# Two of five gate/up pairs per layer as seven products of half blocks

## The chip, the cores and the metric

The kernel runs on one core of a Trainium2 chip. The metric is the device time of one execution in microseconds (us); a number given for a kernel is the median of several runs. The engines of the core are named as the profile names them: PE (TensorE, matmul), PEld (its weight loads), DVE (VectorE), ACT (ScalarE), POOL (GpSimd) and SP (SyncE, which here only issues transfers).

## The reference

A decoder trunk of two layers on 256 tokens of 1024 channels, all in float32. Each layer adds to the residual stream h first a mixer (a retention branch and a Mamba-2 branch, merged by gates), then a dense feed-forward part (FFN):

```
h = h + hybrid_mixer(rmsnorm(h, norm_mix_w[l]), w_in[l], ...)
h = h + swiglu(rmsnorm(h, norm_ffn_w[l]), w_gate_up[l], w_down[l])

def swiglu(h, w_gate_up, w_down):
    gu = h @ w_gate_up                       # 256 x 1024 by 1024 x 5632
    gate, up = jnp.split(gu, [D_FF], axis=-1)   # D_FF = 2816
    return (jax.nn.silu(gate) * up) @ w_down
```

A final rmsnorm follows the two layers. The change concerns only `h @ w_gate_up`.

## The kernel before

**Precision.** A float32 product is made of three matmuls: each factor is split into a high part, rounded to float32r, and a low part, the remainder. `mm3` (lines 339 to 342) adds high x high, high x low and low x high into one accumulator in PSUM. The weights are split on the fly: a piece of weights is brought by a transfer on SP's queue into a tile `raw` (128 partitions x up to 1024 elements, 512 KB); ACT copies it to the high part `wh` (line 324), DVE subtracts to get the low part `wl` (line 331). `feeder` (line 298) issues the loads in the order of the jobs, `splitter` (line 316) does the split. There are four `raw` buffers (RB) and six slots for split pieces (HB, the counter `hlS`). A raw buffer is free again when DVE has split it; a slot is free when PE has used the piece.

**The tokens** are split the same way: a norm (class `Norm`) scales the tokens, PE transposes them by `transposed` (line 375), ACT copies the high part out of PSUM into `xT` (line 387) and DVE subtracts the low part (line 388).

**Jobs of the FFN.** The 5632 columns of `w_gate_up` are five pairs of 512 gate columns and 512 up columns (NPAIR = 5, c = 0 to 4) and a last job with the 256 + 256 columns left. A job of 512 columns (`tm_job`, line 492) has four pieces of two k-blocks (256 of the 1024 rows each). For each of 8 k-blocks and of 2 blocks of 128 tokens it does one `mm3` of 512 columns: 48 matmuls, so 96 for a pair. Pair 0 is ordered so that the first token block goes ahead (`tm_pair`). When a token block of the gate is complete, ACT takes its Silu out of PSUM into a tile `sil` (line 1213); when that of the up part is, DVE multiplies (line 1221), and the product is transposed and split as operand `gu` of the down projection, `out_job(gu, ...)` on line 1249.

**The order of the work.** The program is written as cooperating generators. A planner (class `Flow`, line 61) runs them at build time with a cost for each instruction (`Op`) and hand-over times between engines. When an engine comes free in the plan, the ready operation with the lowest priority value `pr` is emitted next. This fixes the order of instructions on each engine. A job has number j: the split of its pieces has priority j - 0.7, its matmuls j + 0.5, its output work j. On the chip each engine works through its list in order and waits on semaphores.

**Buffers that the change touches.** Four accumulators in PSUM (`accS`), two transposition buffers (`trS`), three `sil` tiles, four `sx` tiles of 512 elements, two `seg` tiles of 1024 elements, four big tiles of tag D; `sx`, `seg` and D serve the mixer and are unused in the FFN.

Of the kernel before, what the change touches and what calls it, by code (L numbers as in the profile page):

```python
# [181 lines left out]
def trunk_kernel(  # L182
# [4 lines left out]
):  # L187
    nc = tc.nc
    HB, RB, TAIL, WARM = 6, 4, 5, 2
    cp = ctx.enter_context(tc.tile_pool(name="cp", bufs=1))  # L190
    wp = ctx.enter_context(tc.tile_pool(name="wp", bufs=HB))
    big = ctx.enter_context(tc.tile_pool(name="big", bufs=4))
# [19 lines left out]
    def tt(n, pr, out, in0, in1, op):  # L212
        return dve(n, pr, lambda: nc.vector.tensor_tensor(out=out, in0=in0, in1=in1, op=op))
# [14 lines left out]
    def pe(cost, pr, fn):  # L228
        return Op("pe", cost, fn, pr)
# [24 lines left out]
    def new_big(tag, dt, shape=(P, 4, SEQ)):  # L254
        return big.tile(list(shape), dt, tag=tag, name=tag, bufs=2 if tag == "xT" else 4)
# [12 lines left out]

    jobs = []
    specs = []  # L270

    def add_job(srcs):
        evs = []
        for src, k, n in srcs:
            ev = Event()
            evs.append(ev)
            specs.append((src, k, n, ev, len(jobs)))
        jobs.append(evs)

    def rows(w, k0, k, n0, n):  # L280
        return ([w[k0 : k0 + k * P, n0 : n0 + n].rearrange("(k p) n -> p k n", p=P)], k, n)
# [5 lines left out]
    def tm_srcs(w, n0, n=512, kper=2):  # L287
        return [rows(w, k0, kper, n0, n) for k0 in range(0, D, kper * P)]
# [7 lines left out]
    first_pieces, rest_pieces = Event(), Event()  # L296

    def feeder():
        for i, (src, k, n, ev, job) in enumerate(specs):
            if i == 2:  # L300
                fl.set(first_pieces)
                yield rest_pieces
            yield rawS

            def load():
                raw = new_raw()
# [7 lines left out]
            fl.spawn(splitter(raw, k, n, ev, job, fl.transfer(512 * k * n)))  # L314

    def splitter(raw, k, n, ev, job, landed):
        yield landed
        yield hlS
        m = k * n
        pr = job - 0.7  # L320
# [12 lines left out]

        wl = yield Op("dve", 1.04 * m + 69, split_l, pr)
        fl.release(rawS)
        fl.set(ev, (wh[:, :m].rearrange("p (k n) -> p k n", k=k), wl[:, :m].rearrange("p (k n) -> p k n", k=k)))


    def mm3(ps, lh, ll, rh, rl, first, last):
        nc.tensor.matmul(ps, lhsT=lh, rhs=rh, start=first, stop=False)  # L340
        nc.tensor.matmul(ps, lhsT=lh, rhs=rl, start=False, stop=False)  # L341
        nc.tensor.matmul(ps, lhsT=ll, rhs=rh, start=False, stop=last)  # L342

    class Operand:


        def __init__(self, n, tags):
            self.n, self.tags = n, tags
            self.parts = [None] * n
            self.ready = [[Event() for _ in range(NT)] for _ in range(n)]  # L350
# [21 lines left out]
            if self.tags[i] != "xT":  # L372
                fl.release(bigS[self.tags[i]])

    def transposed(src, n, dst, i, t, pr):
# [12 lines left out]
        yield tt(n * P, pr, dl, v, dh.bitcast(F32), ALU.subtract)  # L388
        fl.release(trS)
        fl.set(dst.ready[i][t])  # L390

    def power(ms, n, pr, tag, bufs):
        r = sp.tile([P, 2], F32, tag=tag, name=tag, bufs=bufs)
# [18 lines left out]
    class Norm:  # L412


        def __init__(self, w):
# [11 lines left out]
        def half(self, t, n, pr):  # L427

            nsl = slice(n * 512, (n + 1) * 512)
            fl.spawn(self.square(t, n, pr))  # L430
            wb = yield self.wb[n]
            r = yield self.rstd[t]
            yield silS
            xn = new_sil()
            yield stt(512, pr, xn, h[t][:, nsl], r, wb, ALU.mult, ALU.mult)
            self.left -= 1
            if not self.left:
                self.free()
            yield from transposed(xn, 4, self.xT, n, t, pr)
            fl.release(silS)  # L440

        def square(self, t, n, pr):
            nsl = slice(n * 512, (n + 1) * 512)
# [53 lines left out]
    def tm_pair(xT, *members):  # L497

        return tm_jobs(xT, members, [(m, t, k) for t in range(NT) for m, n in ((0, 8), (1, 4)) for k in range(n)]
                       + [(1, t, k) for k in range(4, 8) for t in range(NT)])  # L500

    def fm_job(xT, post):

# [92 lines left out]
    def add_layer_jobs(l):  # L596
        for kind, *at in MIXER:
            if kind == "v":
                add_job(tm_srcs(w_in[l], C_V + 512 * at[0], kper=1 if l == at[0] == 0 else 2))
            elif kind == "gr":  # L600
                add_job(tm_srcs(w_in[l], C_DT + 352 * at[0], 352))
            elif kind == "q":
                add_job(fm_srcs(w_in[l], C_Q + DK * at[0]))
            elif kind == "k":
                add_job(fm_srcs(w_in[l], C_K + DK * at[0]))
            elif kind == "bc":
                add_job(fm_srcs(w_in[l], C_X + 256 * (8 + 2 * at[0] + at[1])))
            elif kind == "xs":
                add_job(fm_srcs(w_in[l], C_X + 256 * (2 * at[0] + at[1])))
            elif kind == "g":  # L610
                add_job(tm_srcs(w_in[l], C_G + 512 * at[0]))
            elif kind == "z":
                add_job(tm_srcs(w_in[l], C_Z + 512 * at[0]))
            elif kind == "gs":
                add_job(tm_srcs(w_in[l], C_GS + 512 * at[0]))
            else:
                add_job(out_srcs({"ret": ret_out, "ssd": ssd_out, "wo": w_o}[kind][l]))
        for c in range(NPAIR):
            add_job(tm_srcs(w_gate_up[l], 512 * c))
            add_job(tm_srcs(w_gate_up[l], FF + 512 * c))  # L620
# [31 lines left out]
    def layer(l, mix, nxt):  # L652
# [517 lines left out]


        mT = Operand(2, ["A", "A"])
        ffn = Norm(norm_ffn_w[l])

        def ssd_post(t, n, ps, j):
            nsl = slice(n * 512, (n + 1) * 512)
# [10 lines left out]
        def ssd_job():  # L1187
            for i in range(2):
                xT.drop(i)
            fl.spawn(ffn.start(at_job[0]))  # L1190
            return out_job(yz, 16, ssd_post)

        run["ssd"] = ssd_job
# [33 lines left out]
        def both_post(t, ps, j):  # L1227
# [6 lines left out]
            yield from transposed(s, n // P, gu, NPAIR, t, j)  # L1234
            fl.release(silS)

        for c in range(NPAIR):
            sg_ev = [Event() for _ in range(NT)]
# [7 lines left out]
        for i in range(2):  # L1246
            ffn.xT.drop(i)
        fl.spawn(nxt.start(at_job[0]))
        yield from out_job(gu, FF // P, add_to(nxt))

# [201 lines left out]
```

## Time and profile before

| what | value |
|---|---|
| median of 3 runs | 1292.29 us (1292.07 to 1292.76) |
| the profiled execution | 1291.82 us |
| its span in the profile | 1290.1 us |
| PE busy | 1279.6 us, 99% |
| DVE busy | 860.5 us, 67% |
| ACT busy | 739.4 us, 57% |
| bytes moved | 237.65 MB, mean 184 GB/s |

The span runs from the first to the last record of the profile; the device time holds 1.7 us more. Engines work at once, so the busy shares add up to more than 100%. Matmuls are pipelined: one is shown with 0.39 us, but the next starts 0.23 us after it. A bracket at the end of a row tells how long the engine idled before it and what ended the idling. The FFN of the first layer runs from 461 to 650 us, that of the second from 1097 us to the end.

### The profile page before, as it was taken

Reading aid. Unit: us, or ns where it says so; the run is one execution under the profiler, and the core shown is the slowest. Engines: PE = TensorE matmul, PEld = TensorE weight load, DVE = VectorE, ACT = ScalarE, POOL = GpSimd, SP = SyncE. Lnnn points to the kernel's source line nnn. Section 1 sums busy time; section 2 is a strip of 40 time slices with the busy share of each in tenths; the row PEclk is TensorE's granted clock in tenths of the full one; section 3 lists DMA queues with packets and bytes.
Section 4 is the critical chain, followed back from the end, with each engine's and each line's share of the span. In section 5 each row is a group of like instructions: output and inputs, shape, how many; then the busy total and the mean of one; then the engine's idle time right before and its main releaser. Section 6 shows DMA issues by size and latency. Waiting matters only on the chain.

```text
span 1290.1 us, 16966 instructions
## 1 busy us (share of the span) xinstructions
PE 1279.6 (99%) x6324; PEld 1075.5 (83%) x6324; DVE 860.5 (67%) x1163; ACT 739.4 (57%) x1086; POOL 35.1 (3%) x57
## 2 busy tenths in 40 slices
PE   9999999999999999999999999999999999999997
PEld 7888888888888888888888988888888888888886
DVE  5875788878575665554478658878876756755544
ACT  5755676886365354444377556966955634544432
POOL 1000000000010000000010000000000100000000
PEclk9999999999999999999999999999999999999999
DMA  7757565556565566665566575656555553766551
GB/s 241 219 168 219 160 192 159 175 194 194 159 216 200 163 198 201 186 194 181 159 199 188 169 205 156 187 182 183 190 168 179 198 210 131 237 187 190 186 188 57
DMA packets 129013, 237.65 MB, mean 184 GB/s; under 512 B 7818, under 2 KB 59906, under 8 KB 128803
## 3 DMA queue, kind: packets, MB, share of 16 engines
q1 hardware_dynamic: 127458, 232.16, 58.1%
q0 software_dynamic: 1472, 4.42, 1.2%
q8 instruction: 49, 0.80, 0.3%
q14 instruction: 34, 0.27, 0.1%
HBM read 235.43 MB, written 1.11 MB: 183 GB/s over the span
## 4 chain that ended last, share of the span: by engine, by line
PE 87%; DVE 4%; ACT 3%; issue 3%; DMA 3%; POOL 0%; SPq 0%; POOLq 0%; DVEq 0%; ACTq 0%
PE acc L340 21%; PE acc L342 21%; PE acc L341 21%; PE acc L521 9%; PE acc L522 5%; PE tr L382 2%; PE yps L1060 2%; DVE wl L331 2%; DMA raw<-in_w_in_dram 1%; PE acc L524 1%; ACT wh L324 1%; ACT seg L1028 1%; PE sm L819 1%; DMA seg<-acs 1%; PE tr L954 0%
## 5 line engine op out<-in xcount | busy, mean ns | idle before, releaser
L331 DVE TENSOR_TENSOR wl<-raw,wh 128x1024 fp32r<-128x1024 f32 (+2 forms) x432 | 514.4, 1194 | 307.9 <-ACT wh L324 305.6
L324 ACT ACTIVATE wh<-raw 128x1024 fp32r<-128x1024 f32 (+2 forms) x432 | 443.8, 1035 | 358.3 <-PE acc L342 277.9
L340 PE MATMUL acc<-wh,xT 128*128 128x512 f32 (+1 forms) x896 | 348.6, 389 | 0.7 <-ACT wh L324 0.5
L341 PE MATMUL acc<-wl,xT 128*128 128x512 f32 (+1 forms) x896 | 343.1, 383 | 0.8 <-DVE wl L331 0.7
L342 PE MATMUL acc<-wh,xT 128*128 128x512 f32 (+1 forms) x896 | 343.0, 383 | 0.0
L521 PE MATMUL acc<-xT,wh 128*128 128x512 f32 x560 | 203.8, 401 | 0.0
L341 PEld LDWEIGHTS acc<-wl,xT 128*128 128x128 f32 x896 | 168.5, 188 | 31.9 <-DVE wl L331 1.9
L340 PEld LDWEIGHTS acc<-wh,xT 128*128 128x128 f32 x896 | 168.5, 188 | 31.8 <-ACT wh L324 0.9
L342 PEld LDWEIGHTS acc<-wh,xT 128*128 128x128 f32 x896 | 168.2, 188 | 31.8
L522 PE MATMUL acc<-xT,wl 128*128 128x256 f32 x640 | 167.2, 281 | 0.0
L522 PEld LDWEIGHTS acc<-xT,wl 128*128 128x128 f32 x640 | 120.9, 189 | 6.9
L521 PEld LDWEIGHTS acc<-xT,wh 128*128 128x128 f32 x560 | 105.5, 188 | 21.3
L340 PE MATMUL acc<-wh,A 128*128 128x512 f32 x192 | 76.7, 400 | 0.0
L216 DVE SCALAR_TENSOR_TENSOR cb<-ca,cv,cb 128x255 f32<-128x255 f32 (+1 forms) x144 | 68.4, 478 | 10.9 <-ACT cb L206 9.8
L342 PE MATMUL acc<-wh,A 128*128 128x512 f32 x192 | 74.9, 390 | 0.0
L341 PE MATMUL acc<-wl,A 128*128 128x512 f32 x192 | 74.8, 390 | 0.0
L340 PE MATMUL acc<-wh,Y 128*128 128x512 f32 x176 | 70.7, 402 | 0.0
L342 PE MATMUL acc<-wh,Y 128*128 128x512 f32 x176 | 68.7, 391 | 0.0
L341 PE MATMUL acc<-wl,Y 128*128 128x512 f32 x176 | 68.6, 390 | 0.0
L340 PE MATMUL acc<-wh,C 128*128 128x512 f32 x128 | 50.6, 395 | 0.0
L342 PE MATMUL acc<-wh,C 128*128 128x512 f32 x128 | 49.9, 390 | 0.0
L341 PE MATMUL acc<-wl,C 128*128 128x512 f32 x128 | 49.8, 389 | 0.0
(141 smaller groups left out, 1295.1 us busy)
## 6 DMA issues: line engine op xcount, KB each, us to landing
raw<-in_w_in_dram SPq DMA_DIRECT2D x188, 512.0 KB, 4.4
raw<-in_w_gate_up_dram SPq DMA_DIRECT2D x80, 512.0 KB, 3.7
raw<-in_w_down_dram SPq DMA_DIRECT2D x44, 512.0 KB, 3.3
raw<-in_ret_out_dram SPq DMA_DIRECT2D x32, 512.0 KB, 4.0
raw<-in_ssd_out_dram SPq DMA_DIRECT2D x32, 512.0 KB, 3.3
raw<-in_w_in_dram SPq DMA_DIRECT2D x24, 352.0 KB, 3.2
seg<-acs SPq DMA_DIRECT2D x16, 512.0 KB, 5.0
raw<-in_w_o_dram SPq DMA_DIRECT2D x16, 512.0 KB, 3.3
```

Of the source, the lines that this page charges most:

```text
L216: return Op("dve", 1.04 * n + 130, lambda: nc.vector.scalar_tensor_tensor(out=out, in0=in0, scalar=scalar, in1=in1, op0=op0, op1=op1), pr)
L324: nc.scalar.activation(out=wh[:, :m], in_=raw[:, :m], func=AF.Copy)
L331: nc.vector.tensor_tensor(out=wl[:, :m], in0=raw[:, :m], in1=wh[:, :m].bitcast(F32), op=ALU.subtract)
L340: nc.tensor.matmul(ps, lhsT=lh, rhs=rh, start=first, stop=False)
L341: nc.tensor.matmul(ps, lhsT=lh, rhs=rl, start=False, stop=False)
L342: nc.tensor.matmul(ps, lhsT=ll, rhs=rh, start=False, stop=last)
L382: nc.tensor.transpose(out=ps[:, j * P : (j + 1) * P], in_=src[:, j * P : (j + 1) * P], identity=ident)
L521: nc.tensor.matmul(a, lhsT=wh[:, k % 4, fsl], rhs=x[:, k % 4, :, :], start=k == 0, stop=False)
L522: nc.tensor.matmul(a[:, :SEQ], lhsT=wl[:, k % 4, fsl], rhs=xh[:, k % 4, :], start=False, stop=False)
L524: nc.tensor.matmul(a, lhsT=wh[:, k % 4, fsl], rhs=x[:, k % 4, :, :], start=False, stop=True)
L819: nc.tensor.matmul(ps[:, :SEQ], lhsT=k[:, b, :P], rhs=q[:, b, :], start=b == 0, stop=b == 1)
L1060: nc.tensor.matmul(ps[:, i * HD : (i + 1) * HD], lhsT=sg[:, i, :], rhs=xdt[:, i * HD : (i + 1) * HD], start=True, stop=True)
```

## The change

In pairs 2 and 4 of each layer (`WINO`) the pair is computed as one 2 x 2 block product by Winograd's form of Strassen's scheme. X is the normed input: its two token blocks are the block rows, the two halves of its 1024 channels the block columns (X11, X12, X21, X22, each 128 tokens by 512 channels). W has the block rows "first and second 512 channels" and the block columns "gate" and "up" (W11, W12, W21, W22, each 512 x 512). Instead of eight block products there are seven, of four k-blocks each, done in this order (`PRODUCTS`), each with three matmuls per k-block:

| product | token operand | weight operand | accumulator |
|---|---|---|---|
| 11 | X11 | W11 | u |
| t1 | X21 - X22 | t1 = W11 + W12 | v |
| t2 | (X21 - X22) - X11 | t2 = t1 + W22 | u, on top of 11 |
| 22 | X12 + that | W22 | c1 |
| t3 | X11 - X21 | t3 = W12 + W22 | u, on top |
| 21 | X12 | W21 | c2 |
| t4 | X22 | t4 = t2 + W21 | u, on top |

- **Weights** (`add_wino`, `wino_sums`): each block comes in two pieces of 1024 elements. W11 is loaded into `seg` tiles and becomes t1, t2 and t4 in place, by three DVE additions per piece. W12 stays in its raw buffer and becomes t3, not by DVE but by a transfer from POOL's queue that reads W22 once more from DRAM and adds it into the tile (`ADDED`). All seven operands are split, so a pair has 14 splits of 1024 elements, where it had 8. The raw buffer of W22 is kept until it is split and t2 is made, that of W21 until it is split and t4 is made.
- **Tokens** (`Norm.sums`, `transposed(..., plain)`): once per layer, behind the FFN's norm, ACT makes four unsplit copies of the transposed tokens in `sx`, DVE makes four differences and sums of 512 elements, each of which is split by ACT and DVE into tiles of tag D.
- **Outputs** (`wino_job`): while PE goes on with other accumulators, ACT copies u out of PSUM after 11, after t2 and after t3; the next product into u waits for that copy. DVE makes two additions for the up part of token block 0, one for its gate part, one for the up part of token block 1. Silu, product, transposition and split follow as before.
- **Order of the splits**: all pieces of the program now take their slots in the order of a list (`turns`).

The core of the diff (the token sums, the output additions and the plumbing of `feeder` and `splitter` are left out):

```diff
+    WINO, ADDED = (2, 4), ("t3",)
+    def wino_sums(i, job, evs, turn, held, part):
+        pr = job - 0.7
...
+        def add(raw, q):
+            yield Op("pool", 1050, lambda: nc.gpsimd.dma_start(
+                out=raw.rearrange("p (k n) -> p k n", k=2), in_=part[q][i], accum_op=ALU.add), pr)
+            yield fl.transfer(512 * D) + 1000.0
...
+        def plus(q, x, raw, src):
+            if q in ADDED:
+                yield from add(x, src)
+            else:
+                w = yield raw
+                yield tt(D, pr, x, x, w, ALU.add)
+            fl.set(used[q])
...
+        x = yield held["11", i]
+        yield from split(x, "11")
+        yield from plus("t1", x, w12, "12")
+        yield from split(x, "t1")
+        yield from plus("t2", x, w22, "22")
+        yield from split(x, "t2")
+        yield from plus("t4", x, w21, "21")
+        yield from last(x, "t4", segS)
...
+    def wino_job(norm, post):
+        def product(q, box, first):
+            xh, xl = yield norm.ops[q]
+            if first:
+                yield accS
+            for k in range(4):
+                wh, wl = yield evs[q][k // 2]
...
+                yield pe(3 * mm_cost(512), j + 0.5, emit)
+                if k % 2:
+                    fl.release(hlS)
...
+        yield from product("11", u, True)
+        fl.spawn(copied(u, silS, new_sil, u1e))
+        yield from product("t1", v, True)
+        u1 = yield u1e
+        yield from product("t2", u, False)
+        fl.spawn(copied(u, sxS, new_sx, u2e))
+        yield from product("22", c1, True)
+        u2 = yield u2e
...
+        yield from product("t3", u, False)
+        fl.spawn(copied(u, sxS, new_sx, u3e))
+        yield from product("21", c2, True)
...
+        u3 = yield u3e
+        yield from product("t4", u, False)
...
         for c in range(NPAIR):
+            if c in WINO:
+                yield from wino_job(ffn, wino_post(c))
+                continue
```

## Rows read from the trace of the kernel before

**Rows 1.** The page: span, then busy us, share and instructions of each engine.
```profile
span 1290.1 us, 16966 instructions
PE 1279.6 (99%) x6324; PEld 1075.5 (83%) x6324; DVE 860.5 (67%) x1163; ACT 739.4 (57%) x1086; POOL 35.1 (3%) x57
```

**Rows 2.** The page: granted TensorE clock in 40 slices, tenths of full speed.
```profile
PEclk9999999999999999999999999999999999999999
```

**Rows 3.** Waits of PE in the whole run: us in total, times, longest.
```profile
PE idle L1332 <- DVE zeros L1305: 1.5, 1, 1.5
PE acc L341 <- DVE wl L331: 0.7, 2, 0.5
PE tr L382 <- DVE sil L216: 0.5, 2, 0.3
PE acc L340 <- ACT wh L324: 0.5, 1, 0.5
PE acc L340 <- DVE Y L213: 0.2, 1, 0.2
```

**Rows 4.** Busy PE, PEld, DVE, ACT, POOL; clock, DMA share, GB/s: pairs 1, 2; 2.
```profile
484.60:507.30 22.70, 22.70 (x105) 18.82 (x104) 12.36 (x13) 10.77 (x12) 0.00 (x0) 1.00 0.69 209
507.30:530.00 22.70, 22.70 (x105) 18.81 (x104) 12.26 (x13) 10.77 (x12) 0.00 (x0) 1.00 0.64 185
...
1142.60:1165.30 22.70, 22.70 (x105) 18.82 (x105) 12.27 (x14) 10.77 (x12) 0.00 (x0) 1.00 0.66 185
```

**Rows 5.** Timeline of PE as pair 2 begins: start us, us, instruction.
```profile
507.55 0.39 PE L341 MATMUL acc<-wl,xT 128*128 128x512 f32 x1
507.77 0.39 PE L342 MATMUL acc<-wh,xT 128*128 128x512 f32 x1
508.00 0.60 PE L382 MATMUL tr<-cst,sil 128*128 128x128 f32 x4
508.36 0.48 PE L340 MATMUL acc<-wh,xT 128*128 128x512 f32 x1
508.67 0.40 PE L341 MATMUL acc<-wl,xT 128*128 128x512 f32 x1
```

**Rows 6.** Timeline of ACT: three splits back to back, then two in pair 1.
```profile
460.42 2.94 ACT L324 ACTIVATE wh<-raw 128x1024 fp32r<-128x1024 f32 x3
...
504.80 1.06 ACT L324 ACTIVATE wh<-raw 128x1024 fp32r<-128x1024 f32 x1 [1.66 <-PE acc L342]
507.52 1.06 ACT L324 ACTIVATE wh<-raw 128x1024 fp32r<-128x1024 f32 x1 [1.66 <-PE acc L342]
```

**Rows 7.** Timeline of DVE between pairs 1 and 2.
```profile
505.89 1.23 DVE L331 TENSOR_TENSOR wl<-raw,wh 128x1024 fp32r<-128x1024 f32 x1 [1.49 <-ACT wh L324]
507.03 1.28 DVE L213 TENSOR_TENSOR sil<-acc,sil 128x512 f32<-128x512 f32 x2
...
509.75 1.34 DVE L213 TENSOR_TENSOR C<-tr,C 128x512 fp32r<-128x512 f32 x2
```

**Rows 8.** Groups by line: operation, tiles, shapes, count, busy us, mean ns.
```profile
L213 DVE TENSOR_TENSOR seg<-seg,cbm 128x1024 f32<-128x1024 f32 x16 | 19.5, 1220 | 2.9 <-ACT seg L206 2.9
L213 DVE TENSOR_TENSOR tail<-tail,xdt 128x512 f32<-128x512 f32 x8 | 5.5, 687 | 0.1
L206 ACT ACTIVATE sil<-acc 128x512 f32<-128x512 f32 x10 | 6.0, 599 | 5.8 <-PE acc L342 5.5
```

**Rows 9.** Landing of the gate/up loads from SP, then of POOL's 512 KB transfers (L405).
```profile
DMA to landing us min/median/max: 2.8/3.7/6.5
...
DMA to landing us min/median/max: 4.2/4.6/6.6
```

**Rows 10.** Timeline at the start of layer 0's FFN, transposes of the second token block.
```profile
467.36 0.63 PE L382 MATMUL tr<-cst,sil 128*128 128x128 f32 x4 [0.25 <-DVE sil L216]
...
468.93 0.68 DVE L213 TENSOR_TENSOR xT<-tr,xT 128x512 fp32r<-128x512 f32 x1
...
471.03 0.39 PE L340 MATMUL acc<-wh,xT 128*128 128x512 f32 x1
```

More of the change, by code (lines that the diff above doesn't have):

```diff
@@ new lines, in new_raw_seg, with holder, land, then @@
+    def new_raw_seg():
+        return new_seg("raws").rearrange("p h i -> p (h i)")
+    def holder(ev):
+        def land(raw, landed):
+            yield landed
+            fl.set(ev, raw)
+        return land
+    def then(land, gens):
+        def run(raw, landed):
+            for g in gens:
+                fl.spawn(g)
+            yield from land(raw, landed)
+        return run
+    def wino_sums(i, job, evs, turn, held, part):
+        pr = job - 0.7
+        def split(raw, q):
+            wh, wl = yield from split_piece(raw, D, turn[q, i], pr)
+            fl.set(evs[q][i], tuple(a.rearrange("p (k n) -> p k n", k=2) for a in (wh, wl)))
+        def add(raw, q):
+            yield Op("pool", 1050, lambda: nc.gpsimd.dma_start(
+                out=raw.rearrange("p (k n) -> p k n", k=2), in_=part[q][i], accum_op=ALU.add), pr)
+            yield fl.transfer(512 * D) + 1000.0
+        def last(raw, q, sem):
+            yield from split(raw, q)
+            fl.release(sem)
+        w12, w22, w21 = (held[q, i] for q in ("12", "22", "21"))
+        used = {q: Event() for q in ("t1", "t2", "t3", "t4")}
+        def plus(q, x, raw, src):
[5 more added lines that the diff above has]
+            fl.set(used[q])
+        def side(ev, q, *sums):
+            raw = yield ev
+            yield from split(raw, q)
+            for a in sums:
+                yield used[a]
+            fl.release(rawS)
+        def third():
+            raw = yield w12
+            if "t1" not in ADDED:
+                yield used["t1"]
+            yield from plus("t3", raw, w22, "22")
+            yield from last(raw, "t3", rawS)
+        fl.spawn(side(w22, "22", *(q for q in ("t2", "t3") if q not in ADDED)))
+        fl.spawn(third())
+        fl.spawn(side(w21, "21", *(q for q in ("t4",) if q not in ADDED)))
+        x = yield held["11", i]
[6 more added lines that the diff above has]
+        yield from last(x, "t4", segS)
@@ L298, in feeder @@
     def feeder():
-        for i, (src, k, n, ev, job) in enumerate(specs):
+        for i, (src, k, n, job, (sem, alloc), land) in enumerate(specs):
             if i == 2:
@@ L313, in feeder, with split_piece @@
             raw = yield Op("sp", 450, load, job)
-            fl.spawn(splitter(raw, k, n, ev, job, fl.transfer(512 * k * n)))
-    def splitter(raw, k, n, ev, job, landed):
-        yield landed
+            fl.spawn(land(raw, fl.transfer(512 * k * n)))
+    def split_piece(raw, m, turn, pr):
+        if turn:
+            yield turns[turn - 1]
         yield hlS
-        m = k * n
-        pr = job - 0.7
+        fl.set(turns[turn])
         def split_h():
@@ L334, in splitter, with land, mm3 @@
         wl = yield Op("dve", 1.04 * m + 69, split_l, pr)
[L335 to L342, printed above, removed]
+        return wh[:, :m], wl[:, :m]
+    def splitter(turn, k, n, ev, job):
+        def land(raw, landed):
+            yield landed
+            wh, wl = yield from split_piece(raw, k * n, turn, job - 0.7)
+            fl.release(rawS)
+            fl.set(ev, tuple(a.rearrange("p (k n) -> p k n", k=k) for a in (wh, wl)))
+        return land
+    def mm3(ps, lh, ll, rh, rl, first, last, **kw):
+        nc.tensor.matmul(ps, lhsT=lh, rhs=rh, start=first, stop=False, **kw)
+        nc.tensor.matmul(ps, lhsT=lh, rhs=rl, start=False, stop=False, **kw)
+        nc.tensor.matmul(ps, lhsT=ll, rhs=rh, start=False, stop=last, **kw)
     class Operand:
@@ L388, in transposed @@
         yield tt(n * P, pr, dl, v, dh.bitcast(F32), ALU.subtract)
+        fl.set(dst.ready[i][t])
+        if plain:
+            yield sxS
+            x = new_sx("plain")
+            yield act(n * P, pr, x.rearrange("p (j t) -> p j t", j=n), v, AF.Copy, psum=True)
+            fl.set(plain, x)
         fl.release(trS)
-        fl.set(dst.ready[i][t])
     def power(ms, n, pr, tag, bufs):
@@ L412, in trunk_kernel, with __init__ @@
     class Norm:
-        def __init__(self, w):
+        def __init__(self, w, sums=False):
+            self.plain = [[Event() if sums else None for _ in range(NT)] for _ in range(2)]
+            self.ops = {q: Event() for q in PRODUCTS}
             self.xT = Operand(2, ["xT", "xT"])
@@ L1245, in layer @@
         yield from tm_job(ffn.xT, both_post)
-        for i in range(2):
-            ffn.xT.drop(i)
+        ffn.drop()
         fl.spawn(nxt.start(at_job[0]))
```

119 lines of the change are left out of this document (111 added, 8 removed).

## The prediction

> **What bounds the kernel now.** I read the busy times first: TensorE (PE) is busy 1279.6 of 1290.1 us, at the full granted clock in every slice [rows 1, 2]. A busy PE is not yet a PE that waits for nothing, so the waits of PE come next: all that it waited for other engines is 3.4 us in the whole run, 1.5 of it before the first job [rows 3]. So what takes work off PE shortens the span, as long as the other engines still deliver in time. For that the stretch of one pair counts, not the average: each gate/up pair lasts 22.70 us with PE busy throughout, DVE 12.3 and ACT 10.8, alike in both layers (two pairs of the first layer, one of the second) [rows 4]. The PE timeline shows why: matmuls start every 0.227 us, and a set of four transposes takes 0.45 us beyond that (507.77 to 508.67, less two such steps) [rows 5]. 96 x 0.227 + 2 x 0.45 = 22.7. The ACT and DVE timelines show the supply: a split starts on ACT when PE frees a slot of the six (504.80, 507.52: one per 2.72 us, the 12 matmuls of a piece) and its second half on DVE ends 2.3 us later [rows 6, 7]. Five pieces thus lie finished ahead of PE, and PE never sees a split in this stretch.
>
> **What goes.** A changed pair has 7 products of 4 k-blocks with 3 matmuls each, 84 for 96 of the same shape, and the same transposes. 12 x 0.227 = 2.72 us less PE per pair; two pairs in each of two layers make 48 matmuls, **-10.9 us**. The pair lasts 20.0 us.
>
> **What comes on the other engines.** Per changed pair 14 pieces are split for 8: six more, and six weight sums on DVE (t1, t2, t4 for two halves). Back to back a split takes DVE 1.14 us (505.89 to 507.03) and ACT 0.94 (2.94 for three less one's own 1.06, halved) [rows 6, 7]. A sum has no row of its own; the 1024-wide tensor_tensor on three SBUF tiles took 1.22 us, as the split does singly [rows 8], so I take 1.14 back to back. Four output adds of 512 (0.69 singly, 0.61 back to back, three SBUF tiles or one PSUM [rows 7, 8]) come to DVE, three copies out of PSUM (0.60 as the Silu there [rows 8]) to ACT. DVE: 20 x 1.14 + 4 x 0.61 + the 2.6 of two products and two second halves that it does per pair now [rows 7] = 27.8 us, against 20.0 of PE. ACT: 14 x 0.94 + 3 x 0.5 + 4 x 0.5 = 16.7, which fits. So inside such a pair DVE is the engine with too much to do, by 7.8 us. Over the pair and the ordinary one beside it DVE needs 27.8 + 11.7 = 39.5 of 42.7 us. The question is whether it can be spread.
>
> **DVE by time.** Let T be the moment when PE starts a changed pair after an ordinary one. Slots come free at T-13.6, -10.9, -8.2, -5.4, -2.7, 0 and then, as PE eats half pieces of 6 matmuls, every 1.36 us. By T five pieces (11 twice, t1 twice, t2) can be split and the four sums of t1 and t2 made: 9 x 1.14 = 10.3 of the 13.6 us, in which DVE has nothing else but its last ordinary splits. The pieces for it are there: the four raw buffers hold both halves of w12 and w22, whose loads (3.7 us median [rows 9]) follow the last ordinary splits, done by T-13.9; the halves of w11 have buffers of their own. From T: the 2.6 us of the pair before, nine splits and two t4 sums, 11 x 1.14 = 12.5, together 15.1. One gap: w21 needs a raw buffer that the split of w22 frees at about T+4.4, so it lands near T+8.5, when DVE has done 2.6 + 5 x 1.14 = 8.3. That ends the last split at about T+15.6. PE needs it when 13 halves are through, T + 13 x 1.36 + 0.9 = T+18.6: **3 us of margin**. The first piece of the next job and the four output adds bring DVE to T+15.6 + 1.1 + 2.4 = 19.1, before T+20.0; two of the adds free the accumulators that the next job starts with. In the ordinary pair behind, DVE has 2.6 + some 16 x 1.14 = 21 us for 22.7, and from T+27 on the slots hold it back again, so pair 4 starts as pair 2 did; after pair 4 come the shared last piece and the down projection, with ordinary splits alone.
>
> **The accumulator u** is written by 11, t2, t3 and t4 in turn, and copied out between them: 11, t1 then t2; t2, 22 then t3; t3, 21 then t4. Each copy has one product's 2.72 us. On ACT at most one split is in front of it (1.06 + 0.60 = 1.7, plus the hand-over), so I take nothing; behind it stand only splits with 6 us to spare. With three splits ahead, 3 x 0.94 + 0.6 = 3.4, PE would stand 0.7 plus hand-overs, about 1.1 us.
>
> **The adding transfer** on POOL: no row shows one. Plain 512 KB transfers from POOL landed after 4.2 to 6.6 us [rows 9]. The lower bound is those; the upper I set at 13.2, twice the longest, since the tile is read as well as written. The first is issued when the t1 sum is made, about T-9.9, the second T-7.2. ACT wants t3 at T+5 to 6.5 in its order; PE is not late until the second comes after T+10.8 (start of its product half at T+13.2 less 2.4 for the two halves of the split). At 6.6 they land by T-0.6: nothing. I take that end, the nearest kind of transfer. At 13.2 side by side nothing either; one after the other the second lands at T+16.5. POOL has nothing else queued there. DMA carries 1.05 MB more in such a pair: 5.2 MB over 20 us is 262 GB/s against 185 at a DMA share of 0.64 [rows 4], a share of 0.91. Landings get later; with the longest load seen, 6.5 us [rows 9], w21's first split ends about T+13.9 and its product starts at T+14.5. That still holds.
>
> **FFN start.** Four plain copies (0.60) on ACT, four differences and four splits of 512 (8 x 0.61 DVE, 4 x 0.5 ACT) per layer. Two copies come ahead of the second token block's norm, 1.2 us at worst on its chain; xT of it is ready at 469.61 and PE takes it at 471.03, 1.4 us later [rows 10]. DVE and ACT idle for about 3 us just behind, and the results are not used for two pairs. I take 0.2 us per layer for transposes queued on PE at their planned place, like the 0.25 there now [rows 10]; bounds 0 and 1.2. In each changed pair I take 0.3 us for the same thing, the longest such wait of the run [rows 3], as DVE comes to its output products without slack; bounds 0 and 2.2 (two late copies of u).
>
> **The sum** from the profiled execution: 1291.82 - 10.9 + 2 x 0.2 + 4 x 0.3 = 1282.5. That execution lies 0.47 below the median of the runs, so the predicted median is **1283.0 us**.
>
> **A rule that speaks against it.** DVE, by the rows, is needed 27.8 us in a stretch that PE would do in 20.0. The Trainium skill, Perfetto Trace Analysis, section Identifying the Most-Contended Engine, says to optimize the engine with the highest occupancy, and its Optimization Strategy section adds that this engine can change between regimes. By that rule, with no spreading between regimes, it is the second rival below; the trace bears out only its first half (PE is that engine now), and shows no stretch of this kind.
>
> **Rivals.** (1) Half gained: u is copied late twice a pair, 2.2 us each time around, or DVE lags as much. -10.9 + 0.4 + 4 x 2.0 = -2.5 at worst, -6.5 for half of that: 1285.8 to 1289.8. For it: engines work in a fixed order, and DVE has little slack. Against: 3 us of margin above. (2) Slower, DVE sets the pair. The place is the nine pieces of work before T: what of it is not done by then is added to DVE's 15.6 behind T. Three us are free by the margin, from 5.7 us on (3.0 + 2.72) the pair is longer than now. With all four sums and the t1 and t2 splits left (7 x 1.14 = 8 us) the loss is 8 - 5.7 = 2.3 per pair, 1292.3 + 9 = 1301; with no spreading at all, 27.8 - 22.7 = 5.1 per pair, 1313. For it: raw buffers are held through two uses. Against: the slot times. (3) Slower by the adding transfer: each us that the second lands after T+10.8 stops ACT, which splits in order, and so PE; past T+13.5 the kernel loses. At T+16.5: 5.7 - 2.7 = 3.0 per pair, 1304. (4) No change: PE pays in hand-overs what it saves, 1292. That needs 2.7 us in each pair, where now it shows 0.
>
> **Chances.** Forecast (1281 to 1285.5) 0.62, (1) 0.20, (2) 0.06, (3) 0.06, (4) 0.06. The low end of the range is no stall at all, 1281.4 less half the spread of the runs, 1280.9; the high end takes in most of (1), 1289.0. Below 1289.7 (0.2%, about what a measurement of this kernel tells from no change) lie the forecast and (1): faster 0.82; within 0.2% the most of (4): 0.05; slower (2), (3) and the rest of (4), 0.13.
>
> **What will show it.** Matmul groups with xT or D fall by 48 in all; a pair of 20.0 to 20.5 us with DVE busy nearly throughout, and a normal one of 22.7 behind it; in the waits of PE at most some tenths at the transposes, nothing on a split; ACT waiting for no adding transfer, and these landed in under 13 us. The prediction is wrong if PE waits for DVE's or ACT's splits by whole microseconds in a changed pair, or for u's copy, or if ACT waits for the adding transfer; and if the mixer's stages, which the change leaves, last longer.

## The result and the profile after

The changed kernel takes 1281.36 us (median of 4 runs, 1280.49 to 1282.07) against 1292.53 us of the kernel before on the same chip (4 runs): a ratio of 0.9911, 95% interval 0.9897 to 0.9925. The prediction was 1283.0 us, range 1280.9 to 1289.0. The profiled execution took 1282.07 us; the sum in the prediction had 1282.5 for it.

The page of the changed kernel, span and busy us with instruction counts, stands against [rows 1]:

```profile
span 1280.3 us, 17056 instructions
...
PE 1268.4 (99%) x6276; PEld 1065.7 (83%) x6276; DVE 931.6 (73%) x1243; ACT 774.5 (60%) x1138; POOL 43.1 (3%) x65
...
PEclk9999999999999999999999999999999999999999
```

PE has 48 instructions fewer and 11.2 us less to do; DVE has 71 us more and ACT 35, and the span is 9.8 us shorter all the same. The granted clock is full in every slice, as in [rows 2], so none of this is the clock.

The waits of PE in the whole run of the changed kernel (us in total, times, longest), against [rows 3]:

```profile
PE tr L486 <- DVE sil L214: 1.6, 4, 0.9
PE idle L1572 <- DVE zeros L1545: 1.5, 1, 1.5
PE acc L445 <- DVE wl L428: 0.7, 2, 0.5
PE acc L444 <- ACT wh L421: 0.6, 1, 0.6
PE acc L444 <- DVE Y L214: 0.3, 1, 0.3
```

The first line is the new one, 1.6 us at four transposes of output products (0.5 us in layer 0, 1.1 in layer 1). The `tr` wait of [rows 3] on line 382 (0.5 us, at the FFN's start) is gone. The other four are those of before.

Windows of the first layer's pairs 1 to 4 in the changed kernel; the columns are those of [rows 4] (busy PE, PEld, DVE, ACT, POOL, then clock, DMA share, GB/s):

```profile
484.40:507.10 22.70, 22.40 (x103) 18.32 (x102) 17.83 (x19) 10.54 (x12) 2.50 (x2) 1.00 0.77 212
507.10:527.10 20.00, 20.00 (x93) 16.55 (x92) 19.41 (x21) 16.17 (x19) 0.00 (x0) 1.00 0.53 175
527.10:549.80 22.70, 22.70 (x105) 18.72 (x104) 20.71 (x21) 12.21 (x14) 2.98 (x3) 1.00 0.92 272
549.80:569.80 20.00, 20.00 (x93) 16.56 (x93) 19.44 (x21) 16.53 (x19) 0.00 (x0) 1.00 0.60 197
```

This is the whole change in four lines. Pairs 2 and 4, by seven products, last 20.0 us with PE busy throughout; the ordinary pairs keep their 22.7. Look at the DVE column: 12.3 us per pair before, now 17.8 in the pair ahead of the first changed one, 19.4 in it, 20.7 in the ordinary pair between the two, 19.4 in the next. The 27.8 us of a changed pair don't stand in one window; they are spread over the neighbours. In the changed pairs DVE has 0.6 us free, in the ordinary pair 3 between them, where it does most (20.7 us), 2.0.

### The profile page after: what moved, and what is told of

The parts are those of the page before. It is cut to its first block, busy times and chain, and to the rows that moved or that the text cites. A ratio compares the mean times of both kernels' runs of the same rounds, so it can differ in the third digit from the quotient of the medians.

```text
span 1280.3 us, 17056 instructions
## 1 busy us (share of the span) xinstructions
PE 1268.4 (99%) x6276; PEld 1065.7 (83%) x6276; DVE 931.6 (73%) x1243; ACT 774.5 (60%) x1138; POOL 43.1 (3%) x65
## 4 chain that ended last, share of the span: by engine, by line
PE 89%; DVE 4%; DMA 3%; issue 2%; ACT 2%; SPq 0%; POOLq 0%; POOL 0%; DVEq 0%; ACTq 0%
PE acc L444 21%; PE acc L446 21%; PE acc L445 21%; PE acc L740 10%; PE acc L741 6%; PE tr L486 2%; DVE wl L428 2%; PE yps L1282 2%; PE acc L743 1%; DMA raw<-in_w_gate_up_dram 1%; ACT wh L421 1%; DMA raw<-in_w_down_dram 1%; DMA raw<-in_w_in_dram 1%; PE tr L1176 1%; PE ips L1269 1%
## 5 line engine op out<-in xcount | busy, mean ns | idle before, releaser
L428 DVE TENSOR_TENSOR wl<-raw,wh 128x1024 fp32r<-128x1024 f32 (+2 forms) x424 | 503.8, 1193 | 216.8 <-ACT wh L421 214.5
L421 ACT ACTIVATE wh<-raw 128x1024 fp32r<-128x1024 f32 (+2 forms) x424 | 434.6, 1034 | 285.9 <-PE acc L446 193.0
L444 PE MATMUL acc<-wh,xT 128*128 128x512 f32 (+1 forms) x816 | 317.1, 389 | 1.0 <-ACT wh L421 0.6
L445 PE MATMUL acc<-wl,xT 128*128 128x512 f32 (+1 forms) x816 | 311.7, 382 | 0.8 <-DVE wl L428 0.7
L446 PE MATMUL acc<-wh,xT 128*128 128x512 f32 (+1 forms) x816 | 311.6, 382 | 0.0
L444 PEld LDWEIGHTS acc<-wh,xT 128*128 128x128 f32 x816 | 153.3, 188 | 28.9 <-ACT wh L421 1.0
L445 PEld LDWEIGHTS acc<-wl,xT 128*128 128x128 f32 x816 | 153.4, 188 | 28.8 <-DVE wl L428 1.9
L446 PEld LDWEIGHTS acc<-wh,xT 128*128 128x128 f32 x816 | 153.2, 188 | 28.7
L217 DVE SCALAR_TENSOR_TENSOR cb<-ca,cv,cb 128x255 f32<-128x255 f32 (+1 forms) x144 | 68.5, 479 | 10.9 <-ACT cb L207 9.8
L421 ACT ACTIVATE wh<-raws 128x1024 fp32r<-128x1024 f32 x32 | 33.6, 1057 | 29.4 <-PE acc L446 24.8
```

Of the source, the lines that this page charges most:

```text
L217: return Op("dve", 1.04 * n + 130, lambda: nc.vector.scalar_tensor_tensor(out=out, in0=in0, scalar=scalar, in1=in1, op0=op0, op1=op1), pr)
```

## Experiments

Each kernel differs from the changed one by the edit shown; the order of the instructions was planned anew each time, with the same costs. Ratios are against the kernel before, on the same chip.

**1. The token sums alone.**

```
-    WINO, ADDED = (2, 4), ("t3",)
+    WINO, ADDED = (), ("t3",)
```

> All five pairs are computed the ordinary way again; the token copies and token sums at the start of each FFN and the new order of taking slots stay, their results unused. Theory A (the gain is 48 matmuls, everything else is hidden): the time of the kernel before, 1292.5 us, plus 0 to 0.4. Rival (the token sums cost what the prediction allowed at most): up to 1294.9, 1.2 us per layer. Rival (part of the gain comes from another order of the work, not from the matmuls): clearly below 1292, by up to 1 us.

Measured: 1291.39 us against 1292.85, ratio 0.9989 (0.998 to 0.9998). With no changed pair the kernel is not slower but 1.5 us faster, by the interval 0.3 to 2.6. If the token sums cost anything, the rest of the edit makes up for it, and a small part of the gain (one eighth, uncertain by nearly its own size) does not come from the matmuls taken out. Its waits of PE have no `tr` wait longer than 0.2 us. The trace does not say where all of it comes from: its span is 1.6 us shorter than that of the kernel before, but 0.7 of this lies ahead of the first FFN (the first instruction of its norm on POOL starts at 454.95 for 455.67), where every engine goes through the same instructions in the same order in both kernels. That much is a difference between two executions.

**2. All four weight sums on DVE** (no adding transfer).

```
-    WINO, ADDED = (2, 4), ("t3",)
+    WINO, ADDED = (2, 4), ()
```

> The sum t3 is made by DVE as the other three; no adding transfer. That puts 2 x 1.14 = 2.3 us more on DVE per changed pair, which then needs 30.1 us. Theory A: both sums are made before the pair starts, in a stretch of 22.7 us where DVE is busy 17.8 in the changed kernel, so they cost PE nothing: 1281 to 1282.5. Rival B (DVE is full at 19.4 of 20.0 us in a changed pair, so what is put on it is paid by PE): 4 x 2.3 = 9 us more, 1290.5. Between: if the w22 buffer is held longer and w21 comes later, up to 1 us per pair, 1285.

Measured: 1288.12 us against 1292.85, ratio 0.9966 (0.9953 to 0.9978). Theory A, mine, missed by 6 us. Two sums of 1.14 us in place of the transfer cost the kernel more than half of its gain. The windows of pairs 2, 3 and 4 in this kernel say where:

```profile
507.10:527.10 20.00, 20.00 (x93) 16.56 (x92) 19.34 (x21) 15.95 (x19) 0.00 (x0) 1.00 0.53 164
527.10:549.80 22.70, 22.12 (x102) 18.06 (x101) 19.88 (x21) 11.20 (x15) 0.00 (x0) 1.00 0.66 226
549.80:569.80 20.00, 17.37 (x79) 13.70 (x78) 19.30 (x20) 14.37 (x17) 0.00 (x0) 1.00 0.49 156
```

Pair 2 is untouched, although its sums are on DVE as well; it is pair 4 that PE cannot keep. So the 3 us of margin inside a pair, by which I had judged, are not the bound. The waits of PE, whole run:

```profile
PE acc L444 <- ACT sil L207: 3.6, 2, 1.8
PE tr L486 <- DVE sil L214: 3.6, 5, 1.5
```

Twice (once per layer) PE stands 1.8 us for a copy of u, the place of rival (1). The chain runs backward from it: PE's matmul, ACT's copy of u, the splits on ACT ahead of that copy, the sum of t2 that the first of them needs. Timelines (start us, us, instruction, in brackets the idle time before it), first PE and ACT:

```profile
559.89 0.50 PE L444 MATMUL acc<-wh,D 128*128 128x512 f32 x1 [1.80 <-ACT sil L207]
```

```profile
549.76 1.06 ACT L421 ACTIVATE wh<-raws 128x1024 fp32r<-128x1024 f32 x1 [3.48 <-DVE raws L214]
...
554.52 1.05 ACT L421 ACTIVATE wh<-raws 128x1024 fp32r<-128x1024 f32 x1
555.47 3.89 ACT L421 ACTIVATE wh<-raw 128x1024 fp32r<-128x1024 f32 x4
559.26 0.58 ACT L207 ACTIVATE sil<-acc 128x512 f32<-128x512 f32 x1
```

Four splits in one stretch (3.89 us) stand right ahead of the copy. In the changed kernel the copy comes at 554.71, between splits that wait for slots and buffers:

```profile
553.74 1.06 ACT L421 ACTIVATE wh<-raw 128x1024 fp32r<-128x1024 f32 x1 [0.27 <-ACT A L207]
554.71 0.58 ACT L207 ACTIVATE sil<-acc 128x512 f32<-128x512 f32 x1
555.18 1.05 ACT L421 ACTIVATE wh<-raw 128x1024 fp32r<-128x1024 f32 x1
```

Counted from the start of the pair's splits, the copy stands behind ten of them here and behind eight in the changed kernel: the order planned anew has put two more, 1.9 us, ahead of it, as much as PE stands. Then DVE in `t3_dve`:

```profile
547.28 1.22 DVE L214 TENSOR_TENSOR raw<-raw 128x1024 f32<-128x1024 f32 x1
548.42 1.22 DVE L214 TENSOR_TENSOR raws<-raws,raw 128x1024 f32<-128x1024 f32 x1
549.55 2.53 DVE L428 TENSOR_TENSOR wl<-raws,wh 128x1024 fp32r<-128x1024 f32 x2
552.00 1.28 DVE L214 TENSOR_TENSOR sil<-acc,sil 128x512 f32<-128x512 f32 x2
553.20 1.21 DVE L214 TENSOR_TENSOR raws<-raws,raw 128x1024 f32<-128x1024 f32 x1
```

The last line is the second sum of t2; in the changed kernel it starts at 547.05, before pair 4 begins at 549.80. Two more sums (the `raw<-raw` line is the second of them) have pushed it behind two splits and the output products of pair 3, which stand next in DVE's order. My new theory: what is short is DVE's time in the one ordinary pair between two changed ones, which pays back for pair 2 and works ahead for pair 4 (call it the debt). It is not short in the sense that DVE is full there: it is busy 19.9 of the 22.7 us of that window.

**3 and 4. The sums on DVE in one of the two pairs only.** The debt says that pair 2's sums on DVE are free, since the pair ahead of it has room, and pair 4's cost the whole loss; a bound inside the pair would treat them alike.

```
     def add_wino(w, n1, n2, ADDED):        # and so handed on to wino_sums
...
-                add_wino(w_gate_up[l], 512 * c, FF + 512 * c)
+                add_wino(w_gate_up[l], 512 * c, FF + 512 * c, ADDED if c == 4 else ())   # dve_in_2
+                add_wino(w_gate_up[l], 512 * c, FF + 512 * c, ADDED if c == 2 else ())   # dve_in_4
```

> t3 made by DVE in pair 2 of each layer, by the adding transfer in pair 4. The kernel with both by DVE took 1288.1 us, 6.8 more than the changed one, and its trace shows pair 2 whole at 20.0 us and pair 4 short of PE work. Theory D (debt: DVE does the sums of pair 2 in time, but the ordinary pair behind has too little DVE time left to work ahead for pair 4 if pair 4 has these two sums as well): 1281.4, at most 1283. Theory B (each us of DVE in a changed pair is paid by PE in that pair): half of the 6.8 us, 1284.8.

> The other way round: adding transfer in pair 2, DVE in pair 4. Theory D: the whole loss is here, 1288 (1286 to 1289). Theory B: 1284.8.

Measured: DVE in pair 2, 1282.88 us, ratio 0.9923 (0.991 to 0.9935); DVE in pair 4, 1287.41 us, ratio 0.9965 (0.9953 to 0.9978), both against 1292.32. The first keeps 9.4 of the 11.2 us, the second loses nearly as much as with both. The trace puts none of the 1.5 us by which the first is behind the changed kernel into its FFNs; the rest of the program runs the same instructions in the same order in both. These are the sums over the two FFN stages (from the first instruction of the FFN's norm on POOL to that of the next norm, windows 455.41:637.60,1085.28:1268.60 of the changed kernel and 456.67:639.92,1087.45:1269.74 of `dve_in_2`):

```profile
sum 365.51, PE 363.81 PEld 299.33 DVE 276.54 ACT 209.76 POOL 13.15; mean PE 181.90 PEld 149.66 DVE 138.27 ACT 104.88 POOL 6.58
sum 365.54, PE 364.05 PEld 299.28 DVE 279.85 ACT 209.61 POOL 8.35; mean PE 182.02 PEld 149.64 DVE 139.93 ACT 104.80 POOL 4.18
```

Pair 4 in the first kernel, then in the second:

```profile
549.80:569.80 20.00, 19.76 (x92) 16.10 (x91) 19.47 (x20) 15.26 (x18) 0.00 (x0) 1.00 0.67 207
```

```profile
549.80:569.80 20.00, 18.17 (x78) 14.56 (x77) 18.71 (x20) 12.72 (x17) 0.00 (x0) 0.91 0.48 158
```

In the second PE again waits twice 1.8 us for u's copy, and the second t2 sum starts at 552.38; the granted clock falls to 0.91 in this window, so a part of its loss is the clock (in `t3_dve` it stayed at 1.00 there). This shows that the transfer is worth something in pair 4 only, where the pair ahead is itself behind a changed one. That the ordinary pair in between decides by its DVE time is argued, not shown: DVE idles for 1.6 us in it in `dve_in_4` too. What tells the kernels apart is ACT's order: wherever PE stood for this copy (pair 4 of both layers, in `t3_dve` and `dve_in_4`) the copy stands behind ten splits, and in every other changed pair of these two, of `dve_in_2` and of the changed kernel behind eight. DVE's lateness and that order come together out of the plan; a kernel with the sums on DVE and the order of the changed kernel, or with pair 4 alone changed, was not run.

**5 and 6. No ordinary pair in between.** If DVE's 27.8 us are hidden only by neighbours, changed pairs side by side must show them.

```
-    WINO, ADDED = (2, 4), ("t3",)
+    WINO, ADDED = (3, 4), ("t3",)          # adjacent
+    WINO, ADDED = (1, 2, 3, 4), ("t3",)    # four_pairs
```

> Pairs 3 and 4 instead of 2 and 4: the same amount of work, without an ordinary pair between. Theory A: last split of pair 4 at 15.6 + 27.8 = 43.4 us after pair 3 starts, wanted at 20.0 + 18.6 = 38.6, so 4.8 us lost per layer: 1291 (1287 to 1294). Rival (where the pairs stand does not matter): 1281.4.

> Pairs 1, 2, 3 and 4 of each layer by seven products. Theory A with the prediction's DVE sum: behind the first changed pair there is no ordinary pair in which DVE could catch up, so each further pair takes DVE's 27.8 us. Last split of pair 4 at 15.6 + 3 x 27.8 = 99.0 us after pair 1 starts, PE would want it at 3 x 20.0 + 18.6 = 78.6: 20.4 us lost per layer against 2 x 2.7 saved, 1281.4 + 2 x 15 = 1311 (1303 to 1316). Rival (PE alone sets the pair, DVE is hidden anyhow): 1281.4 - 10.9 = 1270.5.

Measured: adjacent 1305.3 us, ratio 1.0097 (1.0083 to 1.0111); four pairs 1336.5, ratio 1.0338 (1.0324 to 1.0352), both against 1292.85. The direction is the expected one, the size larger: two pairs side by side lose 24 us against the same two pairs apart, with the same instructions. The stretch of `adjacent` that begins with its second changed pair, and its waits of PE:

```profile
552.50:580.00 27.50, 23.01 (x90) 16.55 (x91) 27.19 (x29) 19.05 (x23) 2.98 (x3) 0.94 0.77 209
```

```profile
PE acc L445 <- DVE wl L428: 7.7, 14, 1.1
PE tr L486 <- DVE sil L214: 5.2, 2, 2.9
PE acc L444 <- ACT wh L421: 3.9, 3, 1.6
```

DVE is busy 27.2 of 27.5 us: here it is the bound. Two windows of `four_pairs`:

```profile
507.10:529.80 22.70, 18.19 (x64) 13.01 (x65) 20.96 (x22) 13.80 (x17) 2.42 (x2) 0.85 0.74 199
508.45:538.26 29.81, 24.90 (x92) 18.24 (x92) 27.96 (x30) 17.66 (x22) 2.42 (x2) 0.89 0.65 175
```

The second line is one period of its pairs, 29.8 us from a DVE split of one pair (508.45) to the same split of the next (538.26). DVE is busy 28.0 us of it, my 27.8, and idle for the other 1.8; and in both kernels the granted clock falls, to 0.94 and 0.85, in windows in which PE stands many times for tenths of a us (32 waits for a split's second half, 16.6 us in all, in `four_pairs`). Both may add to the loss that the DVE sum gives; I did not part them.

**7. One changed pair.**

```
-    WINO, ADDED = (2, 4), ("t3",)
+    WINO, ADDED = (2,), ("t3",)
```

> Only pair 2 of each layer by seven products. If the gain is the matmuls alone: 24 x 0.227 = 5.4 us less than with none, halfway between 1291.4 (none, token sums left in) and 1281.4 (two): 1286.2 (1285.5 to 1287.2). If pair 4 gains less than pair 2 because DVE comes to it in debt: below 1286.

Measured: 1287.34 us against 1292.45, ratio 0.9961 (0.9948 to 0.9974). Pair 2 lasts 20.0 us, pairs 3 and 4 are ordinary ones without a wait of PE. That is 0.1 us above the range expected for the matmuls alone, and not below 1286, as it would be if pair 4 gained less. From experiment 1 (1291.4) the first pair gives 4.0 us, from here to the changed kernel (1281.4) the second gives 6.0, where 24 x 0.227 = 5.4; with runs of one kernel 1.6 to 3.1 us apart the two are not told apart.

**8. A second sum by a transfer.** If DVE's time is what is short, less of it should be no loss.

```
-    WINO, ADDED = (2, 4), ("t3",)
+    WINO, ADDED = (2, 4), ("t3", "t4")
```

> t4 is made by an adding transfer as well as t3, in both pairs of each layer. DVE has 2.3 us less per changed pair, DMA 1 MB more. Theory D (DVE repays its debt in time already): only the last waits of PE behind DVE can go, 1.6 us in the changed kernel's trace; 1280.4 (1279.8 to 1281.6). Theory B (a us of DVE in a changed pair is a us of PE): 4 x 2.3 = 9 us less, 1272. If the second transfer lands too late for the last product, PE waits: 1283 or more.

Measured: 1292.98 us against 1292.45, ratio 1.0002 (0.9993 to 1.0011). The whole gain is lost; both first expectations missed, the third had the sign. Windows of pairs 2 and 4:

```profile
507.10:527.10 20.00, 20.00 (x93) 16.42 (x92) 16.89 (x19) 15.54 (x18) 2.39 (x2) 1.00 0.80 215
...
549.80:569.80 20.00, 17.57 (x81) 14.24 (x81) 14.02 (x15) 12.55 (x16) 2.98 (x3) 1.00 0.84 219
```

DVE has time (14.0 of 20), and PE waits. The transfers themselves are no slower (5.5 to 6.6 us). But DMA's share in pair 2 is 0.80 for 0.53, and the load of w21 comes late; ACT, in its fixed order, waits for it with the next copy of u behind it:

```profile
517.66 1.06 ACT L421 ACTIVATE wh<-raw 128x1024 fp32r<-128x1024 f32 x1 [2.49 <-DMA raw<-in_w_gate_up_dram]
518.63 0.58 ACT L207 ACTIVATE sx<-acc 128x512 f32<-128x512 f32 x1
```

In the changed kernel that split starts at 515.50 after 0.69 us of waiting. From 490 to 600 us ACT waits 12.4 us for gate/up loads here, 4.8 there. PE pays as in experiment 2, at u's copy (`ACT sx`, 4.7 us in three waits) and at the transposes (3.7 us).

**9 and 10. The adding transfer made twice and three times.** t3 then holds its second block two or three times, so the output differs.

```
-            yield Op("pool", 1050, lambda: nc.gpsimd.dma_start(..., accum_op=ALU.add), pr)
-            yield fl.transfer(512 * D) + 1000.0
+            for _ in range(2):      # add_twice; 3 in add_thrice
+                yield Op("pool", 1050, lambda: nc.gpsimd.dma_start(..., accum_op=ALU.add), pr)
+                yield fl.transfer(512 * D) + 1000.0
```

> The adding transfer is made twice, one after the other, into the same tile (t3 then holds W22 twice, so the output of the FFN is not the reference's). One takes 5.9 us from issue to landing; the second of the later half, issued 6 us before the pair, lands about 6 us into it, where ACT splits t3 6.7 us into it. The slack of the prediction (no loss up to 10.8 us into the pair): 1281.4 to 1283. If the transfer has no slack: 6 us per pair, 1305.

> The same three times (t3 holds W22 three times, the output is not the reference's). The last lands about 12.2 us into the pair, past the 10.8 of the prediction: a loss of 1.4 us per pair by that bound, up to 3.2 because DVE's work behind the stopped split has only 2.8 us of margin: 1287 to 1294. If nothing is lost, the slack is larger than stated: 1281.4.

Measured: twice 1285.41 us, ratio 0.9942 (0.9928 to 0.9956); three times 1316.54, ratio 1.0179 (1.0154 to 1.0204), both against 1292.45. So twice the transfer's time costs 4 us, not nothing: both pairs stay at 20.0 us, ACT waits 1.8 us in three waits for the transfer, and what is lost shows at transposes and behind pair 4, with a DMA share of 0.86 to 0.89 in pairs 3 and 4. Three times costs 35 us, where I had expected 13 at most for a pure lateness. ACT's timeline in pair 2 of that kernel shows rival (3) at work:

```profile
517.26 1.06 ACT L422 ACTIVATE wh<-raw 128x1024 fp32r<-128x1024 f32 x1 [4.91 <-DMA raw<-in_w_gate_up_dram]
518.23 0.58 ACT L207 ACTIVATE sx<-acc 128x512 f32<-128x512 f32 x1
521.62 2.96 ACT L422 ACTIVATE wh<-raw 128x1024 fp32r<-128x1024 f32 x3 [2.81 <-DMA raw<-in_w_gate_up_dram]
```

In all ACT waits 36.6 us, in 8 waits, for the adding transfers. The granted clock is 0.94 in the window 507.10:527.10 there, so not all of the 35 us is waiting. So there is a point from which lateness decides, and the changed kernel is less than one transfer's time away from losing something; that this point lies at T+10.8 is not shown.

**11 and 12. The sums of t1, t2 and t4 on POOL.** POOL is idle 97% of the run; this asks if it is a better home for them than DVE.

```
-                yield tt(D, pr, x, x, w, ALU.add)
+                yield pool(D, pr, x, x, w, ALU.add)     # pool_sums
-    WINO, ADDED = (2, 4), ("t3",)
+    WINO, ADDED = (1, 2, 3, 4), ("t3",)                 # pool_sums4, with the line above
```

> Pairs 2 and 4 as in the changed kernel, but t1, t2 and t4 are added by POOL and not by DVE (t3 stays with the adding transfer). DVE needs 6 x 1.14 = 6.8 us less per pair. Theory A (PE is full already): 1281.4, plus or minus 1. Rival (POOL and DVE get in each other's way: POOL's small power instruction took 1.46 us instead of 0.55 where a split ran beside it, so a split may wait as long for a POOL sum of 1 to 4 us): DVE loses 6 to 24 us per pair, 1285 to 1340.

> The same in pairs 1, 2, 3 and 4. DVE then needs 14 x 1.14 + 2.4 + 2.6 = 21.0 us per pair against 20.0 of PE, ACT 16.7. If DVE's amount of work is what made four pairs slow (1336.5 with the sums on DVE, 29.8 us per pair in the trace): 1271 to 1278, faster than the changed kernel. If the raw buffers or POOL set the pair, or POOL and DVE hinder each other: 1290 or more.

Measured: 1328.17 us, ratio 1.0279 (1.0263 to 1.0295), and 1387.49, ratio 1.0736 (1.0721 to 1.0751), both against 1292.32. The groups of `pool_sums` from 484 to 620 us (count, busy us, mean ns, idle before):

```profile
L227 POOL TENSOR_TENSOR raws<-raws,raw 128x1024 f32<-128x1024 f32 x12 | 35.0, 2922 | 76.1 <-DVE wl L428 55.7 <-DMA raw<-in_w_gate_up_dram 20.2
L428 DVE TENSOR_TENSOR wl<-raws,wh 128x1024 fp32r<-128x1024 f32 x16 | 29.0, 1815 | 15.0 <-ACT wh L421 14.9
```

and two lines of its timeline:

```profile
507.46 2.80 POOL L227 TENSOR_TENSOR raws<-raws,raw 128x1024 f32<-128x1024 f32 x1
507.85 3.50 DVE L428 TENSOR_TENSOR wl<-raws,wh 128x1024 fp32r<-128x1024 f32 x1 [3.37 <-ACT wh L421]
```

What PE pays stands in its waits, 30.1 us of them at the output products for 1.6 in the changed kernel:

```profile
PE tr L486 <- DVE sil L214: 30.1, 8, 4.5
```

A sum takes POOL 2.9 us for DVE's 1.2, and a DVE split beside it takes 3.50 for 1.22. The two lines of the timeline show how: POOL's sum ends at 510.26, the split at 511.35, 1.09 us later, which is about one split's own time [rows 7]. The split started second and, by this, stood until POOL was through. With the sums this slow, `pool_sums4` cannot tell whether DVE's amount of work is what made the four pairs slow. The Trainium skill, SBUF — State Buffer, section Who interferes with whom, says this: a DVE instruction with two SBUF inputs contends with a GpSimd instruction that reads SBUF, and the order of issue decides which of them blocks. The trace agrees.

## Why the prediction held, step by step

- **-48 matmuls, 10.9 us**: right. PE lists 48 instructions less, and a changed pair lasts 20.00 us, as worked out. In the profiled executions the account closes: -10.9, +1.6 at the transposes of the output products, -0.5 for the wait at the FFN's start that went, together -9.8, the difference of the spans. That it closes to the tenth is luck: the two FFN stages (365.5 us, and before 374.5, from 455.67 to 642.71 and 1090.94 to 1278.40) are 9.0 us shorter, and the other 0.8 lies in the mixers, where both kernels run the same instructions in the same order.
- **DVE's 27.8 us, spread**: right, but judged at the wrong place. The margin that I worked out holds; DVE in pair 2 of the changed kernel:

```profile
515.99 1.22 DVE L214 TENSOR_TENSOR raws<-raws,raw 128x1024 f32<-128x1024 f32 x1
...
520.60 2.35 DVE L428 TENSOR_TENSOR wl<-raws,wh 128x1024 fp32r<-128x1024 f32 x2
```

  The last two splits (t4) end at 522.95, T + 15.85 with T = 507.10 (predicted T + 15.6); PE starts the last half at 525.74 (T + 18.64, predicted T + 18.6). 2.8 us of margin for 3.0. (The terms that the prediction lists add up to T+15.3, not T+15.6: the gap that it names is 0.2 us.) What it passed over lightly is the ordinary pair behind ("21 us for 22.7"), measured 20.7, in which pair 4's first sums have to be made in time. Experiments 2 to 4 show that the room is ahead of pair 2 and not ahead of pair 4: 2.3 us more on DVE for pair 4 cost 6 us, the same 2.3 us for pair 2 nothing in the FFN stages. The figures were right; that the margin inside the pair decides was not. How far the loss ahead of pair 4 is DVE's time and how far the planned order of ACT stays open.
- **u's copies at nothing**: right in the changed kernel (PE waits nowhere for them), with little to spare: pair 2's first copy ends at 512.55, and PE takes u again at 513.50. Rival (1) names the place where the kernel breaks first: experiments 2, 4 and 8 all lose there, 2 and 4 by splits planned ahead of the copy (1.8 us with four of them, where the prediction put 1.1 for three), 8 by a late load.
- **The adding transfer at 6.6 us**: measured 5.9, inside the bounds. For the changed kernel, its landing and its issue on POOL:

```profile
DMA to landing us min/median/max: 5.9/5.9/6.1
```

```profile
497.91 1.27 POOL L330 DMA_DIRECT2D raw<-in_w_gate_up_dram  x1 [32.65 <-DVE raws L214]
501.06 1.22 POOL L330 DMA_DIRECT2D raw<-in_w_gate_up_dram  x1 [1.87 <-DVE raws L214]
```

  They were issued at T-9.2 and T-6.0 (predicted T-9.9, T-7.2), landed by about T, and ACT did not wait. I had the DMA load heaviest in the changed pair (0.91); it came in the ordinary pair 3 (0.92, the third window above), since loads run ahead as the splits do. The gate/up loads landed after 4.7 us in the median for 3.7.
- **0.3 us per changed pair at transposes**: 1.2 predicted, 1.6 measured.
- **0.2 us per layer at the FFN's start**: wrong in sign, and small. The wait of [rows 10] went, 0.25 us in each layer, and experiment 1 shows the edit without changed pairs to be about 1.5 us faster, not 0.4 slower. The wait's end is seen in the changed kernel's timeline of POOL at the second token block:

```profile
464.71 0.55 POOL L227 TENSOR_TENSOR rstd<-ms,mhalf 128x1 f32<-128x1 f32 x1 [8.75 <-DVE ms L222]
```

  Before, this instruction took 1.46 us (464.97, beside a split on DVE that had begun at 464.81); here it starts 0.01 us before the split at 464.72 and takes 0.55. It looks like the contention of experiment 11, on a tile of one element per partition; no run isolates it. It accounts for 0.5 us of the 1.5; of the rest, experiment 1's trace puts some down to the execution. It may also be why the median came out 1.6 us under the forecast, but the runs of the changed kernel themselves spread by 1.6 us, so this is not shown. The median thus came to the end of the range that stood for no stall at all, 1281.4, although the trace shows 1.6 us of stalls: that it is so near to it is luck. (Of the range and the rivals, two figures do not follow from their own words: the low end takes 0.5 us off for half the spread of the runs, which is 0.35, and rival (1) counts 2.0 us a pair where it says 2.2.)
- **The rule on the most contended engine**: the prediction weighed the Trainium skill, Perfetto Trace Analysis, Identifying the Most-Contended Engine, as the case without spreading. With ordinary pairs in between it did not come so (20.0 us pairs with 27.8 us of DVE work); with none in between it did (29.8 us in `four_pairs`).

No kernel tried here beats the changed one; the nearest has t3 on DVE in pair 2 and the transfer in pair 4 (1282.88 us).

## What to carry to other kernels

Work moved off the bounding engine onto one that has less than its share of free time in that stretch is hidden only as far as the stretches beside it can lend time: add up the helper's work over the changed stretch and the free one between two changed ones, then ask by when each piece must be done, since a window with free time in it can still deliver late. When an engine works in a fixed order, a late input costs through the small, urgent instruction that stands behind it (here a 0.6 us copy of an accumulator), so follow the wait back along the order until something is late by itself, and compare that order between the kernels: a new plan changes it. A transfer that adds, or a sum on an idle engine, is not free room: check what it shares (DMA time, an SBUF port) before counting what it takes off.

## What the runs showed of the hardware

- A 512 KB transfer that adds into its tile landed after 5.9 us (5.9 to 6.1, eight of them) and its issue held POOL for 1.2 us, against 4.6 [rows 9] and 0.57 for a plain one there (which spreads one row of weights over the 128 partitions, so the two differ in more than the addition). The Trainium skill, DMA: Bandwidth & Descriptors, section Anatomy of one DMA — SWDGE (gpsimd) path, fits 2.0 us + bytes / 436e3 per transfer, an estimate of 3.2 us for 512 KB; the runs here show more for both kinds.
- A float32 sum of 1024 elements per partition took POOL 2.9 us in the mean, and a DVE split that began 0.39 us behind one took 3.50 us for 1.22. A one-element instruction on POOL took 1.46 us behind a DVE split and 0.55 ahead of one.
- The granted clock stayed at full level in every slice of the changed kernel, though PE had 1.6 us of new waits; it fell to 0.85 to 0.94 in windows of `four_pairs`, `adjacent` and `dve_in_4`, where PE stood for splits and copies. Not every window with such waits shows it: in pair 4 of `t3_dve` and `t4_too` PE was busy only 17.4 and 17.6 of 20.0 us, at 1.00.
